# Attention scores for two heads at a time in the two halves of TensorE's rows, with TensorE's order written out by hand

## The chip, the cores and the metric

One core of a Trainium2 chip runs the whole program in one launch. The metric is the device time of that launch in microseconds (us). The kernel before takes 2198.34 us (median of three runs, 2196.09 to 2198.70).

## The reference, cut to what matters

A backbone of four layers over 256 latent tokens (a grid 64 wide) and 256 context tokens, width 1024, 16 heads of 64. Layers 0 and 3 mix tokens by attention (slots 0 and 1 of its weights), layer 1 by a Conformer convolution, layer 2 by a short gated convolution; after each comes a squared-ReLU MLP.

```python
def neighbourhood_attention(h_lat, h_ctx, wqkv, wo, rpb, ctx_out):
    q, k, v = split_heads(h_lat @ wqkv, 3)
    q = q * ATTN_SCALE
...
    s_lat = einsum("bhqd,bhaqkd->bhqak", q_r, k_nb) + bias_r
    s_ctx = einsum("bhqd,bhcd->bhqc", q_r, k_c)
    p = softmax(concatenate([s_lat, s_ctx], -1))
    o_lat = (p_lat @ v_nb + p_ctx @ v_c) @ wo
    if ctx_out:
        o_ctx = softmax(q_c @ k_c) @ v_c @ wo
    return o_lat, o_ctx
...
    m_l = modulate(rmsnorm(x, norm2_g[i]), mod_l[:, 3], mod_l[:, 4])
    x = x + mod_l[:, 5] * sq_relu_mlp(m_l, mlp_w1[i], mlp_w2[i])
```

## The kernel before

Every large product is made of three matmuls (mm3, L103): each fp32 operand is split into a part hi of type fp32r, written by ScalarE (L222), and the rest lo, written by VectorE (L223), and hi·hi, hi·lo and lo·hi are summed in PSUM (L106 to L108). Weights come by DMA from SP into four raw tiles (128x1024 each) and are split into tiles of tag w, of which there are ten. PSUM has six tiles of tag mm and two of tag x, one bank each.

Attention (L823 on): layer 0 works on 512 tokens with three units of queries, units 0 and 1 with 128 latent rows each against 512 keys, unit 2 with two blocks of 128 context rows against 256 keys each. Layer 3 has units 0 and 1 alone. For each of eight head pairs (hp) `qk` makes q and k of two heads, 128 rows by 512 tokens (q 256 in layer 3), as 24 matmuls each; it is a generator that yields twice in each (L130 to L147, `tall`). Its results are split by qk_parts (L803), which also copies each head's part into the other half of the rows. attn_pairs (L749) is a second generator, over (hp, unit, head): scores (attn_unit, L697), softmax on VectorE and ScalarE (add of the bias L714, maximum L722, exponential L724, reciprocal L725, product L727), four transposes into a tile of tag x (L736) which ScalarE copies out (L737) two steps later, and four steps after the scores the product with the values (L746), whose two heads write the two halves of PSUM's rows (finish, L760 and L761, splits the sum). The scores take two matmuls for each head: one over 128 rows (q_hi above q_lo, against k_hi twice, L707) and one over the 64 rows of that head (q_hi against k_lo, L708).

```python
        n = 2 * len(units)
        pairs = self.attn_pairs(slot, range(8), q, k, v, o, units)
        rest = (x for hp in range(1, 8) for x in qk(hp))
        for _ in range(3 if layer == 0 else 6):
            next(rest)
        self.interleave(rest, pairs, n, 4)
```

These lines (L857 to L862) mix the two generators, so q and k of a head pair are made beside the attention of the pair before. Then the first half of the output projection wo is mixed with the rest of the attention (first_half), and its second half follows. In this way the program gives an order, but the framework's scheduler then orders each engine's instructions by its own estimate of when operands are there; what it decided is fixed in the built program, and each engine works its queue in that order. Two streams run along: the modulation vectors of later layers, as matmuls (mod_tensor, L372) or on VectorE (mod_vectors, L309 to L330, whose DMAs fill four tiles of tag mraw). A bias tile (L674) is fetched by two DMAs of POOL (L682), masked by POOL (L685), and has two buffers.

Of the kernel before, what the change touches and what calls it, by code (L numbers as in the profile page):

```python
# [8 lines left out]
F32 = mybir.dt.float32  # L9
# [7 lines left out]
P = 128  # L17
# [16 lines left out]
class Net:  # L34
# [75 lines left out]
    def gemm(self, w, segs, acts, cols, evac, k0=0, nk=KT, tall=False, first=False):  # L110

        outs = range(sum(n for _, n in segs) // P)
        each = cols if isinstance(cols, list) else [cols] * len(outs)
        each = [slice(*c) for c in each]
        pss = {}

        def step(d, k, part):  # L120
            if d not in pss:
                pss[d] = self.ps()
            s, c = slice(d * P, d * P + P), each[d]
            self.mm3(pss[d][:, c], (part[0][:, s], part[1][:, s]), (acts[k][0][:, c], acts[k][1][:, c]),
                     k == 0, k == nk - 1)

        block = 8 if tall else 4
        for b0 in range(0, nk, block):
            parts = self.weights(w, k0 + P * b0, block, segs)
            last = b0 + block == nk  # L130
            if first:
                for kk in range(block):
                    for d in outs:
                        step(d, b0 + kk, parts[kk])
                        if last and kk == block - 1:
                            evac(d, pss[d][:, each[d]], each[d])
                    self.tick()
                    yield
            else:
                for d in outs:  # L140
                    for kk in range(block):
                        step(d, b0 + kk, parts[kk])
                        if tall and kk == 3:
                            self.tick()
                            yield
                    if last:
                        evac(d, pss[d][:, each[d]], each[d])  # L147
                    self.tick()
                    yield
# [199 lines left out]
    def mod_tensor(self, layer, vectors):  # L349
# [324 lines left out]
    def bias_tile(self, slot, h):  # L674
# [12 lines left out]
        return e  # L687
# [6 lines left out]

        return self.rows64(ap)[:, :, ::-1]

    def attn_unit(self, q, k, h, unit, e):  # L697

        nc = self.nc
        kh, kl = k
        p = slice(64 * (h % 2), 64 * (h % 2) + 64)
        s = self.ps()

        def scores(out, qc, kc):
            nc.tensor.matmul(out=out, lhsT=q[:, qc], rhs=kh[:, kc], start=True, stop=False)  # L707
            nc.tensor.matmul(out=out, lhsT=q[p, qc], rhs=kl[p, kc], start=False, stop=True)  # L708
        soft = self.tmp()
        nm, sm, ri = self.small()[:, :2], self.small()[:, :2], self.small()[:, :2]  # L710
        if unit < 2:
            scores(s, slice(unit * P, (unit + 1) * P), slice(0, NTOK))
# [3 lines left out]
            groups = [slice(0, 512)]  # L716
        else:
            for i in range(2):
                scores(s[:, i * LAT:(i + 1) * LAT], slice((2 + i) * P, (3 + i) * P), slice(LAT, NTOK))
            groups = [slice(0, 256), slice(256, 512)]  # L720
# [28 lines left out]
    def attn_pairs(self, slot, hps, q, k, v, o, units):  # L749

        nc = self.nc
        items = [(hp, u, hh) for hp in hps for u in units for hh in range(2)]
        bias, soft, pt, out = {}, {}, {}, {}

        def finish(hp):
            ps = out.pop(hp)
# [7 lines left out]
        lag, lag2 = 2, 2  # L764
        todo = []

        def weigh(hp, u, pt):
            if u == 0:
                out[hp] = self.ps()
# [1 line left out]
            if u == units[-1]:  # L771
                finish(hp)

        for i in range(len(items) + lag + lag2):
            if i < len(items):
                hp, u, hh = items[i]
                h = 2 * hp + hh
                if u == 0:
                    bias[h] = self.bias_tile(slot, h)
                soft[i] = self.attn_unit(q[h], k[h], h, u, bias[h])  # L780
            if todo and todo[0][0] == i:
                weigh(*todo.pop(0)[1:])
            if lag <= i < len(items) + lag:
                hp, u, hh = items[i - lag]
                if hh == 0:
                    pt = self.wtile([2, 4, P] if u < 2 else [2, 2, LAT], F32)
                self.attn_transpose(soft.pop(i - lag), u, pt[:, hh])
                if hh == 1:
                    todo.append((i + lag2, hp, u, pt))
            yield  # L790

    def value(self, v, acts, g, tt, i, part, ps):

# [9 lines left out]
    def qk_parts(self, q, k, hp, d, src, c):  # L803

        nc = self.nc
        halves = [slice(0, 64), slice(64, 128)]
        if d == 0:
            for i, p in enumerate(halves):
                x = q[2 * hp + i] = self.hid(F32R)
                hi, lo = self.turned(x[p, c]), self.turned(x[halves[1 - i], c])  # L810
                nc.scalar.activation(out=hi, in_=self.rows64(src[p]), func=AF.Copy, scale=0.125)
                nc.vector.scalar_tensor_tensor(out=lo, in0=self.rows64(src[p]), scalar=0.125, in1=hi.bitcast(F32),
                                               op0=ALU.mult, op1=ALU.subtract)
            return
        low = self.hid(F32R)
        for i, p in enumerate(halves):
            x = self.hid(F32R)
            k[2 * hp + i] = (x, low)
            nc.scalar.activation(out=x[p], in_=src[p], func=AF.Copy)
            nc.vector.tensor_tensor(out=low[p], in0=src[p], in1=x[p].bitcast(F32), op=ALU.subtract)  # L820
            nc.scalar.activation(out=x[halves[1 - i]], in_=src[p], func=AF.Copy)

    def attention(self, layer, slot, cols, then):  # L823
        nc, t = self.nc, self.t
# [523 lines left out]
```

## Time and profile before

| | |
|---|---|
| median of three runs | 2198.34 us |
| the profiled execution, its own time | 2198.73 us |
| its span, first to last instruction | 2196.9 us |
| mean granted TensorE clock | 0.996 |
| TensorE busy | 2168.3 us (99%) |
| VectorE busy | 1543.7 us (70%) |
| ScalarE busy | 868.1 us (40%) |
| POOL busy | 94.6 us (4%) |
| share of TensorE in the chain that ended last | 94% |

The span is one execution seen by the hardware profiler. A matmul's end is modelled in the profile, so what one costs is read from start to start. The chain that ended last is followed back from the last instruction to whatever released each step.

### The profile page before, as it was taken

The page shows a single profiled execution, that of the slowest core. Times are in us where ns is not written, and L with a number is a line of the kernel's source. Part 1 is how long each engine was busy: PE and PEld are TensorE (multiplying, and loading weights), DVE is VectorE, ACT ScalarE, POOL GpSimd, SP SyncE. Part 2 cuts the span into 40 slices and gives each one's busy share as a digit, 9 for nine tenths or more (in the row PEclk, how much of TensorE's full clock was granted, in tenths as well). Part 3 has the DMA queues.
Part 4 walks back from the last instruction along what each step waited for, and adds up shares of the span by engine and source line. Part 5 has one row for each costly group of instructions (what it writes and reads, how often), then busy time and mean ns, then how long its engine had stood idle before and what let it go on. Part 6 is the DMA issues. An engine that isn't in the chain of part 4 may idle for free.

```text
span 2196.9 us, 33176 instructions
## 1 busy us (share of the span) xinstructions
PE 2168.3 (99%) x12900; PEld 1791.8 (82%) x12900; DVE 1543.7 (70%) x2697; ACT 868.1 (40%) x1455; POOL 94.6 (4%) x167
## 2 busy tenths in 40 slices
PE   8999999999999999999999999999999999999998
PEld 5766678888889878888888988888888888778998
DVE  5366558887886957677586988488667566778665
ACT  4355544232233326523223332242322334667444
POOL 1112100000000000000000000000000000230000
PEclk9999999999999999999999999999999999999999
DMA  9555644645543351454454445335456425564653
GB/s 322 151 92 96 132 112 159 187 144 161 168 147 93 118 188 59 155 171 145 123 173 135 144 148 167 98 124 182 133 167 205 132 85 172 77 81 153 192 186 122
DMA packets 202173, 318.62 MB, mean 145 GB/s; under 512 B 14533, under 2 KB 67713, under 8 KB 202016
## 3 DMA queue, kind: packets, MB, share of 16 engines
q1 hardware_dynamic: 198096, 309.78, 44.7%
q0 software_dynamic: 3616, 6.60, 5.0%
q8 instruction: 101, 1.65, 0.3%
q14 instruction: 56, 0.46, 0.1%
q10 hardware_dynamic: 304, 0.12, 0.0%
HBM read 313.67 MB, written 2.78 MB: 144 GB/s over the span
## 4 chain that ended last, share of the span: by engine, by line
PE 94%; DVE 3%; DMA 2%; issue 1%; ACT 1%; POOL 0%; ACTq 0%; POOLq 0%; DVEq 0%; SPq 0%
PE mm L106 28%; PE mm L108 28%; PE mm L107 28%; PE mm L985 2%; PE x L736 2%; PE mm L746 2%; PE mm L708 1%; PE x L372 1%; PE mm L707 1%; DMA e<-in_na_rpb_dram 1%; PE x L491 0%; DMA raw<-in_mlp_w_dram 0%; DVE a L558 0%; DVE w L223 0%; PE x L271 0%
## 5 line engine op out<-in xcount | busy, mean ns | idle before, releaser
L222 ACT ACTIVATE w<-raw 128x1024 fp32r<-128x1024 f32 (+1 forms) x377 | 392.9, 1055 | 666.8 <-PE mm L107 583.7
L223 DVE TENSOR_TENSOR w<-raw,w 128x1024 fp32r<-128x1024 f32 (+1 forms) x377 | 453.1, 1218 | 260.5 <-ACT w L222 258.7
L106 PE MATMUL mm<-a,w 128*128 128x512 f32 (+2 forms) x1792 | 630.2, 352 | 1.4 <-DVE t L630 1.4
L107 PE MATMUL mm<-a,w 128*128 128x512 f32 (+2 forms) x1792 | 627.2, 350 | 0.0
L108 PE MATMUL mm<-a,w 128*128 128x512 f32 (+2 forms) x1792 | 624.7, 350 | 2.0 <-DVE w L223 2.0
L107 PE MATMUL mm<-h,w 128*128 128x256 f32 (+1 forms) x1504 | 506.3, 337 | 0.1
L106 PE MATMUL mm<-h,w 128*128 128x512 f32 (+1 forms) x1376 | 472.4, 343 | 0.0
L108 PE MATMUL mm<-h,w 128*128 128x512 f32 (+1 forms) x1376 | 470.7, 342 | 0.0
L106 PEld LDWEIGHTS mm<-a,w 128*128 128x128 f32 x1792 | 337.4, 188 | 55.6 <-issue 8.0
L108 PEld LDWEIGHTS mm<-a,w 128*128 128x128 f32 x1792 | 337.6, 189 | 49.6 <-DVE w L223 2.5
L107 PEld LDWEIGHTS mm<-a,w 128*128 128x128 f32 x1792 | 338.3, 189 | 46.4 <-DVE t L544 0.8
L107 PEld LDWEIGHTS mm<-h,w 128*128 128x128 f32 x1504 | 283.3, 188 | 32.6 <-DVE h L223 0.3
L317 DVE SCALAR_TENSOR_TENSOR macc<-mraw,cw,macc 128x512 f32<-128x512 f32 x420 | 292.7, 745 | 12.3 <-DMA mraw<-in_mod_w_dram 11.0
L106 PEld LDWEIGHTS mm<-h,w 128*128 128x128 f32 x1376 | 258.9, 188 | 36.5 <-issue 3.9
L108 PEld LDWEIGHTS mm<-h,w 128*128 128x128 f32 x1376 | 258.8, 188 | 33.4 <-issue 0.6
L589 DVE SCALAR_TENSOR_TENSOR x<-mm,mod,x 128x256 f32<-128x256 f32 x288 | 127.2, 478 | 89.8 <-PE mm L108 88.6
L222 ACT ACTIVATE h<-t 128x512 fp32r<-128x512 f32 (+1 forms) x148 | 80.8, 547 | 93.8 <-DVE t L620 76.5
L619 ACT ACTIVATE t<-mm 128x512 f32<-128x512 f32 (+1 forms) x136 | 69.2, 511 | 93.2 <-PE mm L108 92.2
L223 DVE TENSOR_TENSOR h<-t,h 128x512 fp32r<-128x512 f32 (+1 forms) x148 | 86.1, 582 | 23.4 <-ACT h L222 22.8
L620 DVE SCALAR_TENSOR_TENSOR t<-mm,t 128x512 f32<-128x512 f32 (+1 forms) x136 | 78.9, 584 | 33.4 <-ACT t L619 33.0
L557 ACT ACTIVATE a<-t,mod 128x256 fp32r<-128x256 f32 x120 | 53.4, 500 | 60.3 <-DVE t L544 60.2
L724 ACT ACTIVATE t<-mm,s 128x512 f32<-128x512 f32 (+1 forms) x96 | 59.0, 617 | 45.1 <-DVE s L722 44.3
(174 smaller groups left out, 1790.4 us busy)
## 6 DMA issues: line engine op xcount, KB each, us to landing
raw<-in_mlp_w_dram SPq DMA_DIRECT2D x256, 512.0 KB, 4.3
mraw<-in_mod_w_dram SPq DMA_DIRECT2D x272, 256.0 KB, 3.0
raw<-in_mod_w_dram SPq DMA_DIRECT2D x40, 512.0 KB, 4.2
raw<-in_na_wqkv_dram SPq DMA_DIRECT2D x64, 256.0 KB, 4.4
raw<-in_sc_win_dram SPq DMA_DIRECT2D x24, 512.0 KB, 4.8
h<-in_mod_w_dram SPq DMA_DIRECT2D x32, 256.0 KB, 6.4
raw<-in_na_wqkv_dram SPq DMA_DIRECT2D x16, 512.0 KB, 4.3
raw<-in_na_wo_dram SPq DMA_DIRECT2D x16, 512.0 KB, 5.0
```

The costliest lines, as they stand in the source:

```text
L106: mm(out=out, lhsT=a[0], rhs=b[0], start=start, stop=False)
L107: mm(out=out, lhsT=a[0], rhs=b[1], start=False, stop=False)
L108: mm(out=out, lhsT=a[1], rhs=b[0], start=False, stop=stop)
L222: self.nc.scalar.activation(out=hi, in_=src, func=AF.Copy)
L223: self.nc.vector.tensor_tensor(out=lo, in0=src, in1=hi.bitcast(F32), op=ALU.subtract)
L317: nc.vector.scalar_tensor_tensor(out=acc[s], in0=raw, scalar=c, in1=acc[s], op0=ALU.mult, op1=ALU.add)
L557: self.nc.scalar.activation(out=hi[:, c], in_=t, func=AF.Identity, bias=sh)
L589: self.nc.vector.scalar_tensor_tensor(out=x, in0=src[:, o:o + LAT], scalar=self.mod1(layer, m, s, j), in1=x, op0=ALU.mult, op1=ALU.add)
L619: nc.scalar.activation(out=r, in_=src, func=AF.Relu)
L620: nc.vector.scalar_tensor_tensor(out=h, in0=src, scalar=0.0, in1=r, op0=ALU.max, op1=ALU.mult)
L724: nc.scalar.activation(out=soft[:, g], in_=s[:, g], func=AF.Exp, bias=nm[:, i:i + 1], accum_out=sm[:, i:i + 1])
L736: nc.tensor.transpose(out=tp[:, dst * P:(dst + 1) * P], in_=p[:, j * P:(j + 1) * P], identity=self.ident)
```

## The change

- A head pair's scores are made together (attn_scores): three terms (q_hi k_hi, q_lo k_hi, q_hi k_lo), each as two matmuls over 64 rows, head 0 in rows 0 to 63 and head 1 in rows 64 to 127, into two PSUM tiles, in turns. For unit 2 this is done for each block of 256 keys.
- qk_parts writes hi and lo of 128 rows once; the copies into the other half fall away.
- attn_pairs goes over (hp, unit) with two yields: scores of a unit, then the eight transposes of the unit before, then the value products of the unit before. The tall product yields four times instead of twice, and the numbers of the interleaving follow (6 and 12 steps ahead, 8 steps in a head pair).
- From the first of these steps to the end of the attention TensorE's order is that of the program (manual_schedule); the other engines are still ordered by the scheduler.
- Bias tiles are fetched a head pair ahead and share the four mraw tiles; layer 0's mod_tensor sums in a tile of tag mm instead of x.

```diff
@@ gemm
                         if tall and kk == 3:
                             self.tick()
+                        if tall and kk % 2 and kk < 7:
                             yield
@@ mod_tensor
-            ps = self.ps("x")
+            ps = self.ps("mm" if layer == 0 else "x")
@@ bias_tile
-        e = self.work.tile([P, 6, 64], F32, tag="bias", bufs=2, name=self.name("e"))
+        e = self.work.tile([P, 6, 64], F32, tag="mraw", bufs=4, name=self.name("e"))
+        if after is not None:
+            nc.vector.tensor_copy(out=e[:, 0, 0:1], in_=after[:, 0:1].bitcast(F32))
@@ attn_unit, now attn_scores and softmax
-            nc.tensor.matmul(out=out, lhsT=q[:, qc], rhs=kh[:, kc], start=True, stop=False)
-            nc.tensor.matmul(out=out, lhsT=q[p, qc], rhs=kl[p, kc], start=False, stop=True)
...
+        s = [self.ps(), self.ps()]
+        halves = [slice(0, 64), slice(64, 128)]
+        def scores(cols, qc, kc):
+            terms = [(q[0], k[0]), (q[1], k[0]), (q[0], k[1])]
+            for i, (a, b) in enumerate(terms):
+                for hh, p in enumerate(halves):
+                    nc.tensor.matmul(out=s[hh][:, cols], lhsT=a[p, qc], rhs=b[p, kc], start=i == 0, stop=i == 2)
...
+        return [self.softmax(s[hh], unit, groups, es[hh]) for hh in range(2)]
@@ attn_pairs
-        for i in range(len(items) + lag + lag2):
+        for i in range(len(items) + 1):
             if i < len(items):
...
+                soft[i] = self.attn_scores(q[hp], k[hp], u, bias[hp])
             yield
+            if i > 0:
+                hp, u = items[i - 1]
+                pt = self.wtile([2, 4, P] if u < 2 else [2, 2, LAT], F32)
+                for hh, x in enumerate(soft.pop(i - 1)):
+                    self.attn_transpose(x, u, pt[:, hh])
+            yield
+            if i > 0:
+                weigh(*items[i - 1], pt)
@@ qk_parts
+        hi, lo = self.hid(F32R), self.hid(F32R)
+        (q if d == 0 else k)[hp] = (hi, lo)
...
+        nc.scalar.activation(out=hi, in_=src, func=AF.Copy)
+        nc.vector.tensor_tensor(out=lo, in0=src, in1=hi.bitcast(F32), op=ALU.subtract)
@@ attention
-        for _ in range(3 if layer == 0 else 6):
+        in_order = ExitStack()
+        in_order.enter_context(self.tc.manual_schedule(engines={mybir.EngineType.PE}))
+        for _ in range(6 if layer == 0 else 12):
             next(rest)
-        self.interleave(rest, pairs, n, 4)
+        self.interleave(rest, pairs, n, 8)
...
         self.run_all(pairs)
+        in_order.close()
```

How this moves instructions is shown at three places. In these rows mm are PSUM tiles of projections, scores and value sums, x those of the transposes, a the normed tokens, w split weights (and the copied transposes), h the parts of q and k, t the softmax. The changed kernel's lines have other numbers: L713 scores, L747 transposes, L748 their copy, L757 value products, L223 and L224 the split, L735 exponential, L823 the split of k.

TensorE in layer 0, before, where q of the next head pair (mm_1552) begins with newly split weights (w_1539 hi, w_1540 lo):

```order
L736 MATMUL x_1532<-ident,t_1427 128x128 x4
L746 MATMUL mm_1441<-w_1501,v_732 64x256
L372 MATMUL x_1356<-raw_1602,cw 32x512
L736 MATMUL x_1578<-ident,t_1490 128x128 x4
L106 MATMUL mm_1552<-a_304,w_1539 128x512
L107 MATMUL mm_1552<-a_305,w_1539 128x512
L707 MATMUL mm_1565<-h_1231,h_1122 128x512
L708 MATMUL mm_1565<-h_1230,h_1122 128x512
L372 MATMUL x_1356<-raw_1602,cw 32x512
L372 MATMUL x_1356<-raw_1604,cw 32x512 x2
L707 MATMUL mm_1610<-h_1235,h_1125 128x512
L108 MATMUL mm_1552<-a_304,w_1540 128x512
L106 MATMUL mm_1552<-a_306,w_1539 128x512
```

TensorE in layer 0, now, at the same place (mm_1556, w_1543 and w_1544):

```order
L747 MATMUL x_1530<-ident,t_1417 128x128 x4
L747 MATMUL x_1536<-ident,t_1427 128x128 x4
L106 MATMUL mm_1556<-a_304,w_1543 128x512
L107 MATMUL mm_1556<-a_305,w_1543 128x512
L108 MATMUL mm_1556<-a_304,w_1544 128x512
L106 MATMUL mm_1556<-a_306,w_1543 128x512
L107 MATMUL mm_1556<-a_307,w_1543 128x512
L108 MATMUL mm_1556<-a_306,w_1544 128x512
L757 MATMUL mm_1394<-w_1529,v_732 64x256 x2
L757 MATMUL mm_1394<-w_1529,v_737 64x256 x2
L713 MATMUL mm_1571<-h_1278,h_1144 128x512
L713 MATMUL mm_1572<-h_1278,h_1144 128x512
L713 MATMUL mm_1571<-h_1278,h_1145 128x512
L713 MATMUL mm_1572<-h_1278,h_1145 128x512
L713 MATMUL mm_1571<-h_1279,h_1144 128x512
L713 MATMUL mm_1572<-h_1279,h_1144 128x512
L106 MATMUL mm_1556<-a_308,w_1543 128x512
```

Before, the scheduler had put scores and modulation products between the first use of the hi part and that of the lo part; now six projection products stand right behind eight transposes, the value products and the next scores behind these, and the six score matmuls stand in one run.

ScalarE in layer 0, now, in the same stretch (mm_1485 and mm_1486 are the scores that stand on TensorE just ahead, x_1530 and x_1536 the transposes above):

```order
L735 ACTIVATE t_1494,s_1496<-mm_1485,s_1495 128x512
L823 ACTIVATE h_1517<-mm_1437 128x512
L748 COPY w_1529<-x_1530 128x512
L735 ACTIVATE t_1503,s_1505<-mm_1486,s_1504 128x512
L748 COPY w_1529<-x_1536 128x512
L223 ACTIVATE w_1543<-raw_1542 128x1024
L223 ACTIVATE w_1550<-raw_1549 128x1024
```

The split that makes w_1543 stands behind both copies of those transposes and behind both exponentials of the new scores.

TensorE in layer 3, now, in the sixth head pair, where the sums of a modulation vector (red_16612, L331) stand among projection products, six products behind the unit's scores; and VectorE's queue up to what writes them:

```order
L108 MATMUL mm_17873<-a_16286,w_17781 128x512
L331 MATMUL x_17932<-red_16612,mask_78 32x16 x4
L106 MATMUL mm_17873<-a_16288,w_17787 128x512
```

```order
L728 TENSOR_TENSOR mm_17897<-mm_17897,e_17710 128x256
L728 TENSOR_TENSOR mm_17898<-mm_17898,e_17714 128x256
L733 TENSOR_REDUCE s_17907<-mm_17897 128x1
L224 TENSOR_TENSOR a_18402<-mod_14705,a_18401 128x2
L736 RECIPROCAL s_17909<-s_17908 128x1
L733 TENSOR_REDUCE s_17916<-mm_17898 128x1
L738 TENSOR_SCALAR t_17906<-t_17906,s_17909 128x512
L324 STREAM_TRANSPOSE t_17929<-macc_17034 128x512
L736 RECIPROCAL s_17918<-s_17917 128x1
L224 TENSOR_TENSOR a_18404<-mod_14705,a_18403 128x2
L325 TENSOR_REDUCE red_16612<-t_17929 128x16
```

The sums are written behind nearly the whole softmax of the unit whose scores (mm_17897, mm_17898) ended just ahead. In the trace before, these four products (L330 there) start at 1944.0 us without a wait.

## Rows read from the trace of the kernel before

**Rows 1.** The page, section 1: an engine's busy time, share, instructions.

```profile
PE 2168.3 (99%) x12900; PEld 1791.8 (82%) x12900; DVE 1543.7 (70%) x2697; ACT 868.1 (40%) x1455; POOL 94.6 (4%) x167
```

**Rows 2.** Busy time in stretches: us, each engine, PEclk, DMA share, GB/s.

```profile
core 0: us, PE busy (x) PEld busy (x) DVE busy (x) ACT busy (x) POOL busy (x), PEclk, DMA share, GB/s
104.35:304.87 200.52, 200.39 (x1113) 134.95 (x1111) 124.58 (x264) 112.32 (x244) 38.50 (x60) 1.00 0.55 102
338.00:344.40 6.40, 6.26 (x29) 6.29 (x30) 5.28 (x10) 4.27 (x6) 0.00 (x0) 0.50 0.55 167
1869.24:1992.04 122.80, 118.12 (x809) 90.83 (x807) 88.72 (x191) 76.72 (x160) 35.36 (x42) 0.97 0.53 75
1966.00:1969.40 3.40, 3.40 (x15) 2.52 (x16) 2.02 (x6) 2.48 (x6) 1.30 (x2) 0.50 0.51 24
2019.55:2023.00 3.45, 3.45 (x28) 3.39 (x29) 3.45 (x4) 3.45 (x7) 0.00 (x0) 1.00 0.38 106
```

**Rows 3.** Timeline of TensorE around one head's scores in layer 0: start, us.

```profile
108.61 0.39 PE L108 MATMUL mm<-a,w 128*128 128x512 f32 x1
108.84 0.40 PE L707 MATMUL mm<-h,h 128*128 128x512 f32 x1
109.16 0.49 PE L708 MATMUL mm<-h,h 64*128 64x512 f32 x1
109.59 0.50 PE L106 MATMUL mm<-a,w 128*128 128x512 f32 x1
109.92 0.39 PE L107 MATMUL mm<-a,w 128*128 128x512 f32 x1
```

**Rows 4.** The same view in layer 3: transposes and value products.

```profile
1988.06 0.60 PE L736 MATMUL x<-ident,t 128*128 128x128 f32 x4
1988.59 1.09 PE L746 MATMUL mm<-w,v 128*64 128x128 f32 x16
1989.61 0.66 PE L736 MATMUL x<-ident,t 128*128 128x128 f32 x4
```

**Rows 5.** Timeline: the first split of k (VectorE) of head pairs five apart.

```profile
126.22 0.67 DVE L820 TENSOR_TENSOR h<-mm,h 64x512 fp32r<-64x512 f32 x1
...
251.81 0.68 DVE L820 TENSOR_TENSOR h<-mm,h 64x512 fp32r<-64x512 f32 x1 [2.35 <-ACT h L819]
...
1875.19 0.68 DVE L820 TENSOR_TENSOR h<-mm,h 64x512 fp32r<-64x512 f32 x1
...
1951.07 0.67 DVE L820 TENSOR_TENSOR h<-mm,h 64x512 fp32r<-64x512 f32 x1
```

**Rows 6.** Groups by line and shape, layer 0's attention: busy, mean ns, idle before.

```profile
L737 ACT COPY w<-x 128x512 f32<-128x512 f32 x48 | 28.0, 585 | 27.6 <-PE x L736 27.1
L724 ACT ACTIVATE t<-mm,s 128x512 f32<-128x512 f32 x32 | 22.0, 688 | 13.1 <-DVE s L722 12.7
L223 DVE TENSOR_TENSOR w<-raw,w 128x1024 fp32r<-128x1024 f32 x18 | 21.9, 1223 | 5.9 <-ACT w L222 5.8
L722 DVE TENSOR_REDUCE s<-mm 128x1 f32<-128x512 f32 x32 | 21.8, 681 | 0.4
L222 ACT ACTIVATE w<-raw 128x1024 fp32r<-128x1024 f32 x18 | 18.8, 1058 | 0.0
L727 DVE TENSOR_SCALAR t<-t,s 128x512 f32<-128x512 f32 x32 | 16.1, 504 | 0.3
L714 DVE TENSOR_TENSOR mm<-mm,e 128x256 f32<-128x256 f32 x32 | 13.7, 429 | 18.3 <-PE mm L708 16.3 <-issue 1.7
L760 ACT ACTIVATE h<-mm 128x512 fp32r<-128x512 f32 x7 | 4.2, 594 | 2.2 <-PE mm L746 2.2
```

**Rows 7.** Timeline of TensorE: its waits over 1 us, releaser in brackets.

```profile
338.14 0.98 PE L491 MATMUL x<-ones,acc 128*128 128x1 f32 x4 [3.53 <-DVE acc L480]
...
1965.93 1.07 PE L736 MATMUL x<-ident,t 128*128 128x128 f32 x4 [2.17 <-DVE t L727]
...
2019.55 0.36 PE L106 MATMUL mm<-a,w 128*128 128x256 f32 x1 [1.43 <-DVE t L630]
```

More of the change, by code (lines that the diff above doesn't have):

```diff
@@ L672, in window_mask, with bias_tile @@
             nc.gpsimd.tensor_copy(out=self.mask[off:off + 64], in_=m[off:off + 64])
-    def bias_tile(self, slot, h):
+    def bias_tile(self, slot, h, after=None):
         nc = self.nc
-        e = self.work.tile([P, 6, 64], F32, tag="bias", bufs=2, name=self.name("e"))
+        e = self.work.tile([P, 6, 64], F32, tag="mraw", bufs=4, name=self.name("e"))
+        if after is not None:
+            nc.vector.tensor_copy(out=e[:, 0, 0:1], in_=after[:, 0:1].bitcast(F32))
         rpb = self.t["na_rpb"]
@@ L695, in turned, with attn_scores, softmax @@
         return self.rows64(ap)[:, :, ::-1]
-    def attn_unit(self, q, k, h, unit, e):
+    def attn_scores(self, q, k, unit, es):
         nc = self.nc
[L702 to L706, printed above, removed]
-            nc.tensor.matmul(out=out, lhsT=q[:, qc], rhs=kh[:, kc], start=True, stop=False)
-            nc.tensor.matmul(out=out, lhsT=q[p, qc], rhs=kl[p, kc], start=False, stop=True)
-        soft = self.tmp()
-        nm, sm, ri = self.small()[:, :2], self.small()[:, :2], self.small()[:, :2]
-        if unit < 2:
-            scores(s, slice(unit * P, (unit + 1) * P), slice(0, NTOK))
+        s = [self.ps(), self.ps()]
[5 more added lines that the diff above has]
+                    nc.tensor.matmul(out=s[hh][:, cols], lhsT=a[p, qc], rhs=b[p, kc], start=i == 0, stop=i == 2)
+        if unit < 2:
+            scores(slice(0, NTOK), slice(unit * P, (unit + 1) * P), slice(0, NTOK))
+            groups = [slice(0, 512)]
+        else:
+            for i in range(2):
+                scores(slice(i * LAT, (i + 1) * LAT), slice((2 + i) * P, (3 + i) * P), slice(LAT, NTOK))
+            groups = [slice(0, 256), slice(256, 512)]
+        return [self.softmax(s[hh], unit, groups, es[hh]) for hh in range(2)]
+    def softmax(self, s, unit, groups, e):
+        nc = self.nc
+        if unit < 2:
             i0 = 2 if unit == 0 else 0
@@ L715, in attn_unit @@
                                     op=ALU.add)
[L716 to L720, printed above, removed]
+        soft = self.tmp()
+        nm, sm, ri = self.small()[:, :2], self.small()[:, :2], self.small()[:, :2]
         n = len(groups)
@@ L751, in attn_pairs @@
         nc = self.nc
-        items = [(hp, u, hh) for hp in hps for u in units for hh in range(2)]
-        bias, soft, pt, out = {}, {}, {}, {}
+        items = [(hp, u) for hp in hps for u in units]
+        bias, soft, pts, out = {}, {}, {}, {}
         def finish(hp):
@@ L762, in finish @@
             o[hp] = (hi, lo)
-        lag, lag2 = 2, 2
-        todo = []
         def weigh(hp, u, pt):
@@ L772, in weigh @@
                 finish(hp)
-        for i in range(len(items) + lag + lag2):
+        for i in range(len(items) + 1):
             if i < len(items):
[L776 to L789, printed above, removed]
-            yield
+                hp, u = items[i]
+                for p in (hp, hp + 1):
+                    if p in hps and p not in bias:
+                        bias[p] = [self.bias_tile(slot, 2 * p + hh, q[hp][0] if slot == 0 and hp == 0 else None)
+                                   for hh in range(2)]
+                soft[i] = self.attn_scores(q[hp], k[hp], u, bias[hp])
+            yield
+            if i > 0:
[6 more added lines that the diff above has]
+                weigh(*items[i - 1], pt)
     def value(self, v, acts, g, tt, i, part, ps):
@@ L805, in qk_parts @@
         nc = self.nc
-        halves = [slice(0, 64), slice(64, 128)]
+        hi, lo = self.hid(F32R), self.hid(F32R)
+        (q if d == 0 else k)[hp] = (hi, lo)
+        hi, lo = hi[:, c], lo[:, c]
         if d == 0:
[L808 to L813, printed above, removed]
-            return
[L815 to L821, printed above, removed]
+            hi, lo, src = self.turned(hi), self.turned(lo), self.rows64(src)
+            nc.scalar.activation(out=hi, in_=src, func=AF.Copy, scale=0.125)
+            nc.vector.scalar_tensor_tensor(out=lo, in0=src, scalar=0.125, in1=hi.bitcast(F32),
+                                           op0=ALU.mult, op1=ALU.subtract)
+            return
+        nc.scalar.activation(out=hi, in_=src, func=AF.Copy)
+        nc.vector.tensor_tensor(out=lo, in0=src, in1=hi.bitcast(F32), op=ALU.subtract)
     def attention(self, layer, slot, cols, then):
```

## The prediction

> **What bounds the kernel now.** I first read the page's busy times: TensorE works 99% of the span [rows 1]. The stretches of the two attention stages come next, since nothing else changes. In layer 0, from the first score to the last value product, TensorE is busy 200.39 of 200.52 us at full clock, while VectorE works 124.6 and ScalarE 112.3 [rows 2]: the stage is bounded by what TensorE is given to do. In layer 3 it is busy 118.12 of 122.80 us, at a mean clock of 0.97 [rows 2]. The 4.7 us are waits for a softmax, of which one of 2.17 us is shown [rows 7]; after it TensorE ran at 0.50, its lower level of 1.2 GHz, for 3.4 us [rows 2]. A mean of 0.97 over 122.8 us is 3.7 us lost, so about two such stretches. A head pair takes 25.1 us in layer 0 ((251.81 - 126.22) / 5) and 15.2 us in layer 3 [rows 5].
>
> **What is taken off TensorE.** Start to start, a projection product of 512 columns takes 0.23 us; the score over 128 rows takes 0.32, the one over 64 rows 0.43, and the projection after them 0.33 [rows 3]. So a change between 128 rows and 64 costs about 0.1 for the product before it, which runs out, and 0.1 for the one after it, whose weights load in the open. A head's scores of one unit cost 0.32 + 0.43 + 0.10 = 0.85 us, two heads' 1.70.
>
> The new six matmuls over 64 rows have no row. Their price has two bounds. One after the other, each takes 0.23: 6 x 0.23 + 0.2 = 1.6 us. Side by side, three turns of some 0.24: 0.92 us. The nearest row to the second is that of the value products, which use the two halves of the columns: sixteen of 128 columns take 1.02 us, where four transposes of 128 columns take 0.53 [rows 4]. One after the other the sixteen would take 1.7, so they run two at a time. I take 0.92, the row halves being no less apart than the column halves.
> The Trainium skill, page "TensorE: Matmul & The Clock Gate", section "Part 3: Packing small matmuls", states that four row tiles gave 3.07 times the rate of one, not 4. No trace shown here has row tiles. An estimate by that page (each pair a third dearer) adds 0.21 us to each of 40 units, some 8 us, and the time below would be 2226.
>
> Counted from the two orders, the changes of mode fall from 186 to 86 in layer 0 and from 88 to 52 in layer 3. The columns of the scores fall too: 64 of 512 and 64 of 256 columns become 48 and 48 pairs in layer 0 (22.1 to 17.1 us at 0.23 for 512), and 64 of 512 become 48 pairs in layer 3 (14.8 to 11.4). Going through every slot of both orders with these prices, TensorE's own work falls by 28.8 us in layer 0 (5.0 of columns, 0.24 for each change of mode, a lone 64-row product paying both sides) and by 9.6 us in layer 3 (3.4 and 0.17). Layer 3's old waits and low clock go with the old order, 4.7 + 3.7: there 18 us in all.
>
> **What is put on TensorE: waits.** TensorE's order is now fixed, and two things stand in it before their operands.
>
> *Layer 0, the projection behind the transposes.* The six products on w_1543 stand right behind eight transposes. I count from the end of the scores ahead. TensorE gets there after six projection products and the transposes, 6 x 0.23 + 0.1 + 8 x 0.11 = 2.4 us. ScalarE's queue has, before the split that it waits for: the first exponential, which needs on VectorE 2 x 0.43 (bias) + 0.68 (maximum) and some 0.25 of hand-over, so starts at 1.8 and takes 0.69; the split of k, 0.59; a copy, 0.59; the second exponential, 0.69; the second copy, 0.59; the split itself, 1.06 [rows 6]. That ends at 6.0, so TensorE waits some 3.65 us. In every second head pair four modulation products stand ahead and cover 0.9 of it. The third product needs the lo part, 1.22 us of VectorE later [rows 6], of which two products cover some 0.4: 0.85 more. In every second head pair the value products wait 0.75 for copies that stand behind two exponentials. Mean 4.4 us a head pair; six of them make 26.5, and I take off 3 because the first unit has no copies ahead. At the stage's end (transposes and value products next to each other, late splits for wo) the same sums give 8.5. Layer 0: 23.5 + 8.5 = 32 us of waits.
>
> *Layer 3.* Here eighteen products and the transposes, 5.1 us, stand between the scores and the new weights, but both exponentials, both copies and the split stand ahead of them, and the copies wait for the transposes: ready at 6.4. That is 1.3 us, and 1.1 for the lo part, since two products of 256 columns cover little. Five head pairs: 12 us. In the sixth the sums of a modulation vector are wanted 1.5 us after the scores, and VectorE gives them behind two additions, two maxima, a product (2 x 0.43 + 2 x 0.68 + 0.50 [rows 6]), the wait for the first exponential of some 0.9, and a transposition and a reduction of 512 columns at about 0.7 (taken from the maximum's 0.68): TensorE waits some 4.0. The rest of the end: 2.8 for a copy behind this, 4.8 for wo's split, 2.0 for the last copies. Together 13.6; layer 3 has 25.6 us of waits.
>
> *The clock.* After waits of 3.53 and 2.17 us TensorE ran at 0.50 for 3.4 us or longer; after one of 1.43 it stayed at 1.00 [rows 2, 7]. Layer 0's waits of 2.7 and 3.65 are of the first kind. 3.4 us at half speed cost up to 1.7; some 0.5 of it falls where TensorE would wait for the lo part anyway. I take 1.2 in six head pairs, 7.2 us, and 1.7 once in layer 3. The bounds are nothing and 1.7 for each of some ten long waits, 17.
>
> **What costs nothing.** The dropped copies of q and k leave 2.3 us a head pair on ScalarE (four of 0.59, by [rows 6]) and are counted in the queues above. Bias tiles are asked for a head pair ahead, 15 us or more before use, so the ring that they now share with the loads of mod_vectors is late only if SP's queue holds these up; SP's order of weights moves by a few loads alone, and a late weight would lengthen the waits above. The modulation sums in a tile of tag mm leave the transposes both x tiles; six mm tiles hold a projection, two scores, a value sum and this.
>
> **The sum.** Layer 0: -28.8 + 32 + 7.2 = +10.4. Layer 3: -18 + 25.6 + 1.7 = +9.3. The profiled execution took 2198.73 us, 0.4 above the median: 2198.7 + 19.7 - 0.4 = **2218 us**.
>
> **Rivals.**
> *The waits are half as long: faster.* Chains of eight hand-overs add up every small error, and the order before also had copy, split and projection close together without any wait of TensorE in layer 0 [rows 2]. With 16 and 12.8 us of waits, and layer 0's below the two that cost the clock: -28.8 + 16 - 18 + 12.8 = -18, so 2180 us. Against it: every link is a row, and the queues are fixed. The point where it decides: a wait before w_1543 under 2 us. With no waits at all it would be 2152. Chance 0.27.
> *The row halves don't overlap: slower still.* Each unit then costs 0.68 more, 24 units in layer 0 and 16 in layer 3 make 27, of which some 3 fall on later waits: 2242 us. For it: no row shows row halves. Against it: the column halves [rows 4]. Chance 0.17.
> *An even trade.* Four fifths of the summed waits (46 of 58) and no low clock take back just the 46.8 saved: 2198 us. Chance 0.09.
> That the order is not what the change says is excluded: the rows of the built program show pairs of scores and the fixed pieces.
>
> **How the numbers follow.** My forecast has what is left, 0.47. Faster by over 0.2% (4.4 us, about what measurements of this kernel can tell) is the first rival, 0.27; within 0.2% the third, 0.09; slower the forecast and the second, 0.64. The range reaches from the first rival's 2180, below which I leave half of its chance, to 2243 just above the second. The forecast's own range is 2203 (waits a tenth shorter, no low clock but in a few places) to 2232 (waits a tenth longer, the clock's upper bound).
>
> **What would show it.** In the profile after: six score matmuls of a unit in about 0.9 us, start to start, head 0 and head 1 a few ns apart (second rival: each 0.23 apart). TensorE's waits in layer 0 at the first projection product behind transposes, released by ScalarE's split, of 2.7 to 3.7 us and behind it one of 0.85 released by VectorE's; a head pair of 25.5 to 27 us; a granted clock under 1 in this stage. In layer 3 a head pair of 16.7 us and a wait of some 4 us of the modulation product for VectorE's reduction. I am wrong if these waits are under 2 us or TensorE is busy throughout while the stage is shorter.

## The result, and the profile after

The changed kernel takes 2220.36 us (median of four runs, 2216.70 to 2222.05), the kernel before in the same comparison 2198.52 (2196.09 to 2202.72): a ratio of 1.0095, 95% interval 1.0083 to 1.0107. It is slower by about 1%, where 2218 was forecast. The profiled execution took 2222.05 us, its span is 2220.3 against 2196.9.

TensorE is busy a little less in a longer span; the page's first section of the changed kernel, to be held against [rows 1]:

```profile
PE 2154.6 (97%) x12996; PEld 1789.1 (81%) x12996; DVE 1520.5 (68%) x2669; ACT 828.5 (37%) x1391; POOL 96.4 (4%) x167
```

Busy time by stretch, from the first score to the start of the last value product of either attention stage, as in [rows 2]:

```profile
core 0: us, PE busy (x) PEld busy (x) DVE busy (x) ACT busy (x) POOL busy (x), PEclk, DMA share, GB/s
105.60:315.20 209.60, 188.49 (x1183) 131.80 (x1182) 113.01 (x251) 95.13 (x218) 29.25 (x48) 0.94 0.43 99
1881.50:2015.00 133.50, 115.61 (x842) 91.52 (x842) 87.14 (x188) 61.63 (x136) 31.19 (x36) 0.95 0.43 82
```

Layer 0's stage grew from 200.5 to 209.6 us, layer 3's from 122.8 to 133.5. In layer 0 TensorE is 12 us less busy and idle for 21, and its clock, 1.00 before, is 0.94 on the mean. The rest of the program differs by 3.6 us (1.2 before the first stage, 2.0 between the stages, 0.4 behind); between the stages it moves from 1562.5 to 1567.5 us over all kernels measured here, so that part is scatter.

Where the waits stand, by the view of waits of TensorE over the whole program (what waited, what released it; us in total, times, longest):

```profile
PE mm L106 <- ACT w L223: 22.2, 12, 3.0
PE mm L108 <- DVE w L224: 12.5, 15, 1.6
...
PE x L331 <- DVE red L325: 5.0, 3, 3.9
```

The first two are waits for the hi and the lo part of split weights, 31.6 of their 34.7 us in the two stages; in the kernel before, neither was among TensorE's waits there. The timeline of TensorE in the changed kernel shows one of them, in the second head pair of layer 0, what it does to the clock, and the next one:

```profile
128.33 1.04 PE L747 MATMUL x<-ident,t 128*128 128x128 f32 x8
132.34 0.80 PE L106 MATMUL mm<-a,w 128*128 128x512 f32 x1 [2.98 <-ACT w L223]
...
134.19 0.63 PE L106 MATMUL mm<-a,w 128*128 128x512 f32 x1
134.62 0.63 PE L107 MATMUL mm<-a,w 128*128 128x512 f32 x1
...
160.19 0.50 PE L106 MATMUL mm<-a,w 128*128 128x512 f32 x1 [2.40 <-ACT w L223]
161.45 0.50 PE L108 MATMUL mm<-a,w 128*128 128x512 f32 x1 [0.53 <-DVE w L224]
```

The eight transposes are followed by the first product on newly split weights, which waits 2.98 us for ScalarE's split; after it a projection product takes 0.43 us from start to start instead of 0.23. In the stretches around the end of this wait and of the one of 3.90 us in layer 3 the clock stands at its lower level of 1.2 GHz (columns as above):

```profile
131.80:138.80 7.00, 6.42 (x20) 3.27 (x20) 2.90 (x3) 2.03 (x3) 0.00 (x0) 0.53 0.44 151
1968.00:1974.60 6.60, 4.80 (x23) 4.14 (x24) 2.60 (x10) 1.15 (x5) 0.02 (x1) 0.50 0.01 2
```

And the scores, which did become cheaper. The timeline around the first unit:

```profile
105.25 0.39 PE L108 MATMUL mm<-a,w 128*128 128x512 f32 x1
105.56 0.95 PE L713 MATMUL mm<-h,h 64*128 64x512 f32 x6
106.44 0.50 PE L106 MATMUL mm<-a,w 128*128 128x512 f32 x1
```

Six matmuls of 512 columns take a slot of 0.88 us (0.92 was forecast, 1.6 if the halves did not overlap); by [rows 3] two heads cost 1.70.

Layer 3, the same view: the split of q's weights, and the sums of the modulation vector.

```profile
1901.16 0.38 PE L106 MATMUL mm<-a,w 128*128 128x256 f32 x1 [1.03 <-ACT w L223]
1902.73 0.39 PE L108 MATMUL mm<-a,w 128*128 128x256 f32 x1 [1.07 <-DVE w L224]
...
1969.80 0.31 PE L331 MATMUL x<-red,mask 128*32 128x16 f32 x8 [3.90 <-DVE red L325]
```

### The profile page after: what moved, and what is told of

Its sections match the earlier page's. It is cut to its first block, busy times and chain, and to the rows that moved or that the text cites. A ratio compares the mean times of both kernels' runs of the same rounds, so it can differ in the third digit from the quotient of the medians.

```text
span 2220.3 us, 33271 instructions
## 1 busy us (share of the span) xinstructions
PE 2154.6 (97%) x12996; PEld 1789.1 (81%) x12996; DVE 1520.5 (68%) x2669; ACT 828.5 (37%) x1391; POOL 96.4 (4%) x167
## 4 chain that ended last, share of the span: by engine, by line
PE 88%; DVE 3%; ACT 2%; issue 1%; DMA 0%; DVEq 0%; ACTq 0%
PE mm L106 26%; PE mm L108 26%; PE mm L107 26%; PE mm L757 2%; PE mm L991 2%; PE mm L713 2%; PE x L747 1%; DVE w L224 1%; ACT w L223 1%; ACT w L748 1%; ACT t L735 1%; PE mm L373 0%; PE x L492 0%; DVE a L559 0%; PE x L529 0%
## 5 line engine op out<-in xcount | busy, mean ns | idle before, releaser
L224 DVE TENSOR_TENSOR w<-raw,w 128x1024 fp32r<-128x1024 f32 (+1 forms) x377 | 455.2, 1226 | 287.6 <-ACT w L223 286.6
L223 ACT ACTIVATE w<-raw 128x1024 fp32r<-128x1024 f32 (+1 forms) x377 | 392.2, 1055 | 674.8 <-PE mm L107 589.8
L106 PEld LDWEIGHTS mm<-a,w 128*128 128x128 f32 x1792 | 338.9, 189 | 82.8 <-ACT w L223 20.9
L108 PEld LDWEIGHTS mm<-a,w 128*128 128x128 f32 x1792 | 339.5, 190 | 59.6 <-DVE w L224 12.8
L223 ACT ACTIVATE h<-t 128x512 fp32r<-128x512 f32 (+1 forms) x148 | 80.9, 547 | 92.9 <-DVE t L621 75.5
L224 DVE TENSOR_TENSOR h<-t,h 128x512 fp32r<-128x512 f32 (+1 forms) x148 | 86.4, 584 | 23.2 <-ACT h L223 22.8
L735 ACT ACTIVATE t<-mm,s 128x512 f32<-128x512 f32 (+1 forms) x96 | 59.2, 620 | 105.7 <-DVE s L733 99.5
```

The source lines that it names most:

```text
L106: mm(out=out, lhsT=a[0], rhs=b[0], start=start, stop=False)
L108: mm(out=out, lhsT=a[1], rhs=b[0], start=False, stop=stop)
L223: self.nc.scalar.activation(out=hi, in_=src, func=AF.Copy)
L224: self.nc.vector.tensor_tensor(out=lo, in0=src, in1=hi.bitcast(F32), op=ALU.subtract)
L735: nc.scalar.activation(out=soft[:, g], in_=s[:, g], func=AF.Exp, bias=nm[:, i:i + 1], accum_out=sm[:, i:i + 1])
```

## The experiments

Theory A: the waits come from the places at which the fixed order wants newly split weights (and one modulation sum). Its rivals: the new grouping of scores, softmax and transposes overloads ScalarE and VectorE wherever TensorE's work stands; any order that is the program's own waits as much; the row halves do not give what they should. Ten kernels were run. The table has their medians, the ratio to the kernel before with its interval, and the length of the two attention stages in the profiled execution.

| kernel | us | ratio (95%) | layer 0 | layer 3 |
|---|---|---|---|---|
| before | 2198 | 1 | 200.5 | 122.8 |
| the change | 2220.36 | 1.0095 (1.0083 to 1.0107) | 209.6 | 133.5 |
| e1, scheduler orders TensorE | 2184.79 | 0.9938 (0.9924 to 0.9953) | 185.7 | 123.0 |
| e2, one head, then the other | 2214.98 | 1.0083 (1.0066 to 1.0099) | 205.8 | 131.8 |
| e3, split early | 2188.60 | 0.9955 (0.9940 to 0.9969) | 185.1 | 130.7 |
| e4, old scores, fixed order | 2212.62 | 1.0066 (1.0049 to 1.0083) | 211.1 | 122.5 |
| e5, e1 and split early | 2179.54 | 0.9913 (0.9898 to 0.9928) | 180.1 | 122.5 |
| e7, fixed in layer 0 alone | 2178.51 | 0.9908 (0.9891 to 0.9924) | 180.4 | 121.1 |
| e8, e5 without loads in layer 3 | 2173.79 | 0.9889 (0.9875 to 0.9904) | 180.0 | 113.9 |
| e9, the change one step later | 2183.21 | 0.9930 (0.9914 to 0.9947) | 183.6 | 126.4 |
| e10, the change without loads in layer 3 | 2221.03 | 1.0111 (1.0092 to 1.0130) | 209.6 | 128.1 |
| e11, before without loads in layer 3 | 2206.44 | 1.0034 (1.0023 to 1.0045) | 202.1 | 122.1 |

**e1: who orders TensorE.**

```diff
-        in_order.enter_context(self.tc.manual_schedule(engines={mybir.EngineType.PE}))
```

> The changed kernel without the fixed order: the framework's scheduler orders TensorE in the attention stages again; scores, bias tiles and the program are those of the change. Theory A (the waits come from the place in TensorE's order where the new weights are first used, and the scheduler puts other work there): most of the 29 us of waits for splits in the changed kernel go, the granted clock of layer 0's attention returns to 0.99 or more, and the time is 2165 to 2185 us, below the kernel before. Theory B (the waits come from ScalarE's and VectorE's load under the new grouping of scores, softmax and transposes, whatever TensorE's order): TensorE waits as long elsewhere, 2210 to 2225 us.

All of the change but the order stays. 2184.79 us, inside theory A's range, at its upper edge. In the profile TensorE's waits for splits over the whole program fell from 34.7 to 4.5 us (1.4 for the hi part, 3.1 for the lo part), and layer 0's clock is back:

```profile
105.70:291.40 185.70, 182.86 (x1181) 127.61 (x1182) 111.74 (x251) 94.88 (x218) 29.55 (x48) 1.00 0.48 111
```

So layer 0's waits belong to the fixed order. Layer 3, with 123.0 us, is only back where it was before: something else holds it there.

**e4: the fixed order alone**, on the kernel before.

> The kernel before with one part of the change alone: TensorE's order in the attention stages fixed to the program's, with the old scores, old interleaving and two bias buffers. If any order that is the program's own makes TensorE wait for splits and softmax, it is slower than before by 10 us or more (over 2208 us). If it is only the change's place of the new weights behind the transposes, the time is within 6 us of before's 2198.

Slower by 15 us, against theory A in its narrow form: the old scores in the program's own order wait for splits too, 1.63 us at a time in layer 0.

```profile
158.53 0.50 PE L106 MATMUL mm<-a,w 128*128 128x512 f32 x1 [1.63 <-ACT w L222]
```

Together with e1 this makes a square: the change without its order is worth -13 us, the fixed order alone +15, both +22. Their sum would be +2; the other 20 us come from the two together: in layer 0 the old scores' order has 13.5 us of waits and one stretch at the lower clock, the changed kernel's 20.9 us and six.

**e3: split early.** The fixed order stays; the weights of the next head pair are fetched and split in the middle of k's product.

```diff
+                            if d == 1 and early is not None:
+                                early()
...
+        def qk_weights(hp):
+            split[hp] = self.weights(w, 0, 8, [(hp * P, P), (D + hp * P, P)])
```

> The changed kernel with its fixed order, but the split of the next head pair's weights written two steps earlier in the program (in the middle of k's product), so that it stands on ScalarE and VectorE ahead of the exponentials and copies that it stood behind. Theory A: layer 0's waits of 2.3 to 3.0 us for the split and their low clock go, likewise layer 3's of about 1; waits at the ends of the stages stay (some 20 us): 2175 to 2190 us. Theory B: the two splits, 2.1 us on ScalarE, push back exponentials and copies, and TensorE waits as long at transposes and value products: 2210 to 2225 us.

Theory A holds in layer 0: no wait for a split is left there until wo's weights, and 209.6 became 185.1 us by this edit alone. In layer 3 theory B holds: the splits now stand ahead of the copies, and the value products wait (timeline of TensorE, layer 3):

```profile
1887.70 1.57 PE L759 MATMUL mm<-w,v 128*64 128x128 f32 x16 [2.07 <-ACT w L750]
```

**e9: the same program, one step later.** It moves the use instead of the split.

```diff
-        for _ in range(6 if layer == 0 else 12):
+        for _ in range(5 if layer == 0 else 11):
```

> The changed kernel with its fixed order and one pair of numbers changed: 5 and 11 steps of the projection ahead instead of 6 and 12. In layer 0 the new weights' first products then stand behind the value products and the next unit's scores, 1.9 to 3.3 us later on TensorE, where by the sums of the prediction the split is ready (wait for the hi part 0 to 0.5 us, for the lo part up to 0.6). Theory A (the place of this one use is the cost): layer 0's attention falls from 209.6 to 183 to 190 us with its clock back at 0.99 or 1.00, layer 3 to 122 to 130, and the time to 2183 to 2196 us. Theory B (any fixed order waits as long somewhere): over 2205 us, as with the old scores in a fixed order.

2183.21 us: two numbers are worth 37 us. Of the five waits of 2.28 to 2.98 us for the split of q's weights in layer 0 none is left; the first for a split is in front of wo's, the 2.9 in these two rows (the waits by the view above, then layer 0's stage):

```profile
PE mm L106 <- ACT w L223: 3.7, 2, 2.9
...
103.10:286.70 183.60, 176.78 (x1177) 128.31 (x1176) 112.11 (x249) 93.44 (x219) 29.42 (x48) 0.98 0.46 115
```

The clock is 0.98 and not the 0.99 expected: a wait of 1.82 us for an exponential at the start of the stage and the one for wo's split each have a stretch at the lower level behind them. This is the sharpest test of the prediction's sum, since operands and the fixed order are kept, and the new weights are used later by the 1.9 to 3.3 us that the sum asked for. What moves with them is the whole attention, by one step against the projections; that this use alone gives the 37 us is not shown.

**e2: do the halves have to alternate?**

```diff
-            for i, (a, b) in enumerate(terms):
-                for hh, p in enumerate(halves):
+            for hh, p in enumerate(halves):
+                for i, (a, b) in enumerate(terms):
```

> The changed kernel with the six score matmuls of a unit in another order: the three of head 0, then the three of head 1, so that neighbours use the same row half. If the halves run side by side only when neighbours alternate, a unit's slot grows from 0.88 to about 1.55 us, 40 units make 27 us, of which a part falls on waits that follow: 2238 to 2247 us. If alternating gives nothing (the gain is in the fewer changes of mode alone), the time stays within 4 us of the changed kernel's 2220.

Neither range was met: it is 5 us faster than the change. It is not slower, so alternating is not what lets the halves run side by side. The windows on these matmuls alone (busy, count, clock, DMA) show why; the first two are the first 60 ns of the first unit's scores and the 0.25 us after, the last two the same of the second unit:

```profile
104.14:104.20 0.06, 0.05 (x2) 1.00 0.83 214
104.20:104.45 0.25, 0.25 (x2) 1.00 1.00 283
108.00:108.05 0.05, 0.04 (x1) 1.00 1.09 164
108.05:108.30 0.25, 0.25 (x1) 1.00 0.57 180
```

In the first unit two matmuls run from the start, though head 1's first stands fourth in the order: TensorE starts it beside head 0's. In the second unit only one runs, because head 1's PSUM tile was not yet free; its three came later by themselves.

```profile
108.01 0.95 PE L713 MATMUL mm<-h,h 64*128 64x512 f32 x3
109.23 0.95 PE L713 MATMUL mm<-h,h 64*128 64x512 f32 x3 [0.27 <-ACT t L735]
```

So the gain comes from using both halves in one run; alternating adds nothing when both tiles are free. Of the 5 us 3.8 lie in layer 0, where the waits for the hi part are 12.4 us in sum against 15.2; why they are shorter was not pursued.

**e5 and e7: both mends.** e5 is e1 with e3's early split; e7 fixes the order in layer 0 alone, with the early split, wo's first weights split early too.

> Both mends together: the new scores, TensorE ordered by the scheduler, and the split of the next head pair's weights two steps earlier. If the two mend the same wait, this adds little to either alone (2185 and 2189): 2178 to 2188 us, layer 0's attention 180 to 186 us, layer 3's 118 to 125. If they mend different waits, the gains add up and it is near the 2160 to 2172 us that the scores' saving without new waits would give.

> Order fixed in layer 0 alone, the early split in both layers, and the first weights of wo also split two steps early. Theory A (each wait at newly split weights can be taken away by writing the split earlier): layer 0's attention falls from 185 to about 180 us, since the waits of 2.4 and 0.5 us in front of wo go, and layer 3 is as with the scheduler, 118 to 125 us: 2174 to 2184 us. Theory B (earlier splits only move the wait to exponentials and copies): layer 0 stays at 185 us or more, 2184 to 2192.

Both give 180 us in layer 0 at full clock (TensorE busy 179.2 of 180.1 in e5), so a fixed order is no worse than the scheduler's once the split is early enough. The two get there differently: e7 has 3.9 us of waits in this stage and e5 0.8, so without waits the fixed order is the shorter one. The early split on the kernel before was not run. Layer 0 of e7:

```profile
105.40:285.80 180.40, 176.41 (x1183) 128.23 (x1182) 112.29 (x251) 95.04 (x218) 29.16 (x48) 1.00 0.51 115
```

Layer 3 stays at 121 to 123 us. There VectorE waits for loads (timeline of VectorE in e5):

```profile
1877.83 0.75 DVE L320 SCALAR_TENSOR_TENSOR macc<-mraw,cw,macc 128x512 f32<-128x512 f32 x1 [4.27 <-DMA mraw<-in_mod_w_dram]
...
1912.69 0.75 DVE L320 SCALAR_TENSOR_TENSOR macc<-mraw,cw,macc 128x512 f32<-128x512 f32 x1 [4.32 <-DMA mraw<-in_mod_w_dram]
```

and the waits of SP's own queue (SPq) say for what these loads (L312) wait (us in total, times, longest): a bias tile of the shared ring, until the addition (L730) has read it.

```profile
SPq L312 <- DVE mm L730: 22.4, 4, 12.4
```

**e8, e10, e11: no such loads in layer 3's attention.** `self.rate` is how much of a background step the program grants at each tick; at 0 the steps of mod_vectors stand still until the head pairs are done. The same edit on e5, on the change and on the kernel before:

```diff
+        rate = self.rate
+        if layer > 0:
+            self.rate = 0.0
...
+        if layer > 0:
+            self.rate = 2 * rate
         self.sq_begin(True)
```

> The scores by scheduler with the early split (e5), and in layer 3's attention the steps of mod_vectors are held back until the head pairs are done. It asks whether the shared ring of four tiles is what keeps layer 3 at 122 us: there VectorE waited 11.5 us for loads of modulation weights that themselves waited for bias tiles to come free, and the softmax stood behind them in VectorE's queue. If so, layer 3's attention falls to 112 to 118 us and the time to 2170 to 2177. If the softmax chain itself sets layer 3's pace, the stage stays within 2 us of 122 and the time at 2177 to 2182, since the held work comes back behind the stage.

> The changed kernel as it is, fixed order and all, with one thing taken out of layer 3's attention: the steps of mod_vectors are held back until the head pairs are done (as in e8). If the prediction's place is right, its wait of 3.9 us in front of the modulation product and the low clock of 6.6 us after it go, with up to 3.7 us of VectorE's waits for loads: layer 3's attention from 133.5 to 123 to 128 us, 3 us come back behind it, 2211 to 2216 us. If those waits only hid the others (splits for q and wo), layer 3 stays above 130 us and the time at 2219 or more.

> The kernel before with the same steps held back in layer 3, to see what of e8's 114 us in that stage is the hold and what the scores. There VectorE waited 19.7 us for bias tiles of its own two buffers and TensorE 4.7 us for a softmax. If the hold alone gives it, layer 3 falls below 118 us and the time is 2191 to 2196; if it needs the new scores, the stage is 120 to 124 us and the time 2197 to 2203.

On e5 layer 3 falls to 113.9 us, of which 3 come back behind the stage (208.0 us there against 205.1): 2173.79 us, the fastest kernel of the study, 1.1% below before. The windows of e8:

```profile
105.80:285.80 180.00, 179.03 (x1181) 128.75 (x1182) 111.70 (x251) 94.96 (x218) 29.00 (x48) 1.00 0.52 115
1849.80:1963.70 113.90, 110.83 (x844) 89.12 (x844) 85.24 (x185) 64.14 (x139) 28.36 (x36) 1.00 0.54 96
```

The eight operations fed by these loads do not leave the stage: they stand at its end, from 1943.8 to 1959.4, and wait 0.2 us for loads where those of e5 waited 11.5. What leaves it is two transpositions and two reductions. The runs do not tell the moved place from the wait that is gone.

On the change the edit takes 5.4 us from the stage (the wait of 3.90 goes, and with it the stretch at the lower clock around it; the one at wo's weights is 6.8 us long there instead of 3.4), but 4.0 come back behind it. Layer 3's 128.1 us lie just above the 123 to 128 expected, and the time, 2221.03, lies with the other case, 2219 or more: what the hold gains in the stage is not gained in the whole.

On the kernel before, the stage hardly moves and the time rises by 8 us, more than expected: 5.1 behind the stage, 1.6 in layer 0, the rest between the stages, where kernels scatter. But this run cannot tell what the hold is worth to the old scores, since there the eight operations stand ahead of layer 3's attention already (it begins at 1869.24). It is the change that moves them into it (timeline of VectorE, first and last of the eight, before and then the change):

```profile
1832.81 0.48 DVE L313 TENSOR_SCALAR macc<-mraw,cw 128x512 f32<-128x512 f32 x1 [1.77 <-DMA mraw<-in_mod_w_dram]
1840.17 0.75 DVE L317 SCALAR_TENSOR_TENSOR macc<-mraw,cw,macc 128x512 f32<-128x512 f32 x1 [0.62 <-DMA mraw<-in_mod_w_dram]
...
1893.07 0.49 DVE L314 TENSOR_SCALAR macc<-mraw,cw 128x512 f32<-128x512 f32 x1 [0.49 <-DMA mraw<-in_mod_w_dram]
1946.46 0.75 DVE L318 SCALAR_TENSOR_TENSOR macc<-mraw,cw,macc 128x512 f32<-128x512 f32 x1
```

Giving the bias tiles a ring of their own was not tried.

## Why the prediction was right, and where its terms were not

**The mechanism** was the one named: the first use of newly split weights behind the transposes, the wait for ScalarE's split, the low clock after it. e3, which moves the split, and e9, which moves the use, take most of layer 0's loss away. The change itself took 26.7 us a head pair in layer 0 ((259.41 - 125.95) / 5, starts of the first unit's scores), the value that the prediction's terms give; in layer 3 it took 17.4 ((1963.34 - 1893.93) / 4), where 16.7 was named.

```profile
125.95 0.95 PE L713 MATMUL mm<-h,h 64*128 64x512 f32 x6
...
259.41 0.97 PE L713 MATMUL mm<-h,h 64*128 64x512 f32 x6
```

**The size** came out through errors that cancel, and that is luck. Measured terms stand beside the forecast: the waits by adding the brackets of the timeline (fifteen in each stage), the clock as half of the time that TensorE was busy at the lower level in the changed kernel, the work as what is left.

| | forecast | measured |
|---|---|---|
| layer 0: work | -28.8 | 209.6 - 20.9 - 11.5 - 200.5 = -23.3 |
| layer 0: waits | +32 | +20.9 |
| layer 0: clock | +7.2 | +11.5 |
| layer 3: work, old waits and clock | -18 | 133.5 - 17.6 - 5.9 - 122.8 = -12.8 |
| layer 3: waits | +25.6 | +17.6 |
| layer 3: clock | +1.7 | +5.9 |
| sum of both | +19.7 | +19.8 |

With its waits alone put right, the prediction's sum would be -28.8 + 20.9 + 7.2 - 18 + 17.6 + 1.7 = +0.6 us: the even trade, not a slower kernel. A third of the waits did not come, and what made up for them was work that fell by less and a clock that cost twice as much as was taken.

*Work.* The step that went through every slot gave too much in both layers. e7 has the same fixed order in layer 0 and few waits: 180.4 - 3.9 = 176.5 us, 24.0 below before and within 1 us of the table, and 21.9 a head pair ((235.31 - 125.94) / 5). The term that was too large is the price of a change of mode, 0.24 us. By the shapes of the matmuls in the traces layer 0's stage has 84 changes in e7, 97 in e5 and 118 in e1; without their waits these stages take 176.5, 179.3 and 183.0 us, so a change costs some 0.2, if nothing else in the three orders counts. The prediction's own counts, 100 changes and 5.0 us of columns, give -25.0 at that price. In layer 3 before's own work was 122.8 - 4.7 - 3.4 = 114.7 us (two stretches of 3.4 at half speed) and the change's is 110.0: it fell by 4.7, half of the 9.6 summed. Why was not worked out.

*Layer 0's waits.* The sum gave 3.65 us, or 2.7 where modulation products stand ahead, in turns. They stand ahead of four of the five: these waits are 2.40, 2.40, 2.28 and 2.40 us, the one without them 2.98, and the one at wo's weights 2.68. So each was 0.3 to 0.7 shorter than summed, mostly below the 2.7 to 3.7 named as the sign, and above the 2 us below which the prediction would have been wrong. For the lo part 0.53 were measured instead of 0.85, and for value products 0.29 and 0.31 in the whole stage instead of 0.75 in every second head pair.

*Layer 3's waits.* 1.03, 1.37, 0.93 and 0.72 us for the hi part (forecast 1.3), 1.07, 0.76, 1.58 and 0.76 for the lo part (1.1), 3.90 for the modulation sum (4.0; the terms written for it add up to 3.5, so the match is partly chance). The first two kinds came in four head pairs and not five, 8.2 us instead of 12. The end of the stage was oversized: six waits of 5.5 us together, the longest of 2.43, stand where 9.6 were summed.

*The clock.* In the changed kernel each wait of 2.28 us and more in the two stages has a stretch at the lower level around or behind it. So have two waits of 1.03 and 1.07 us close to each other in layer 3, for which the prediction took nothing by its row of 1.43. The first stretch and the sum of six in layer 0, then the first and the sum of three in layer 3:

```profile
131.58:138.41 6.83, 6.03 (x18) 3.24 (x20) 2.52 (x4) 2.25 (x3) 0.00 (x0) 0.50 0.44 152
sum 23.88, PE 22.95 PEld 12.31 DVE 7.45 ACT 4.26 POOL 0.00; mean PE 3.83 PEld 2.05 DVE 1.24 ACT 0.71 POOL 0.00
...
1903.10:1906.51 3.41, 3.41 (x24) 2.68 (x24) 2.16 (x3) 0.38 (x1) 0.66 (x1) 0.50 0.59 173
sum 13.65, PE 11.78 PEld 9.63 DVE 5.71 ACT 1.65 POOL 0.73; mean PE 3.93 PEld 3.21 DVE 1.90 ACT 0.55 POOL 0.24
```

Half of the 22.95 and 11.78 us is 11.5 and 5.9, together the upper bound of 17 that was given and not the 8.9 taken. A head pair of layer 0 says the same: it costs 26.7 - 21.9 = 4.8 us more than in e7, its waits are 2.8 on the mean, and 2.0 are left for the clock, where 1.2 was taken.

*What cost nothing.* The shared ring of four tiles was said to be late only if SP's queue held it up. That step failed: it is the loads of mod_vectors that wait for bias tiles, 14.7 us in the change's layer 3, and the eight operations that they feed stand inside that stage now. For TensorE this stayed small in the change (VectorE waited 3.7 us for such loads in layer 3); once the splits were early it was part of what set layer 3's pace.

*The rivals.* That the row halves do not overlap is refuted by the slot of 0.88 us. The Trainium skill's 3.07 for four row tiles (page "TensorE: Matmul & The Clock Gate", "Part 3: Packing small matmuls") would have made a pair a third dearer; the slot shows nothing of this for two. Waits half as long, 28.8 us in sum, were not met in the change, but the 38.5 measured lie nearer to them than to the 57.6 forecast, and e9 shows how near the outcome was: one step later in the order, and the time lies on that rival's side. The even trade wanted 46 us of waits and no low clock; the change had fewer waits and the low clock.

## What to carry to other kernels

When an order is fixed by hand, each first use of a freshly made operand needs its own sum: the queue of the engine that makes it, from the event that starts that queue, against the work that the fixed order puts in between. A late operand is then best mended by writing its maker earlier or its use later by one step, before the work itself is made cheaper; here two numbers were worth 37 us, and the new scores under the scheduler's order 13. After each mend, look again at what ends last: in layer 3 the late splits hid a ring of buffers shared by two streams.

## What the runs showed of the hardware that was not expected

- Matmuls of the two row halves need not alternate. With three of one half ahead of three of the other, the fourth started beside the first, and the slot stayed 0.89 us (104.15 to 105.04 in e2).
- The low clock can outlast the wait that it follows: around a wait of 2.98 us that ended at 132.34, TensorE stood at a mean granted clock of 0.53 for 7.0 us.
- The length of one wait does not settle the clock. Of five waits of 1.63 us in layer 0 of e4 one was followed by a stretch at 0.50, two of 1.03 and 1.07 in layer 3 of the change were, and in layer 0 of e11, where TensorE has no wait, the clock fell all the same (windows of e11, all engines). What else decides was not found.

```profile
112.90:116.39 3.49, 3.49 (x20) 2.50 (x19) 2.06 (x8) 2.30 (x6) 0.80 (x1) 1.00 0.66 34
116.39:119.80 3.41, 3.41 (x11) 2.73 (x11) 2.40 (x5) 1.69 (x6) 1.78 (x2) 0.50 0.56 32
```
